# u and z of a chunked gMLP layer by seven block products, with v's norm moved into the v stage

## The chip, the cores and the metric

The kernel runs on one core of a Trainium2 chip. The metric is the device time of the program in microseconds. The tensor engine (PE) multiplies, VectorE (DVE) and ScalarE (ACT) do elementwise work, GpSimd (POOL) a few small steps, and SyncE (SP) issues the DMAs. The arrays live in three large tiles: arF (float32) and arR (float32r, the operands of matmuls) on chip, and arP, the eight PSUM banks of 512 columns.

## The reference

Two layers work on 128 prompt and 512 sample tokens (640 in all) of width 1024. The first is latent attention, the second, which the change touches, a gMLP mixer of width 2048:

```python
def chunk_mlp(h, w_in, v_g, v_b, w_s, b_s, w_o):
    b, t, _ = h.shape
    proj = h @ w_in
    uv = jax.nn.gelu(proj[..., :2 * MLP_WIDTH])
    z = proj[..., 2 * MLP_WIDTH:]
    u, v = uv[..., :MLP_WIDTH], uv[..., MLP_WIDTH:]
    v = layernorm(v, v_g, v_b).reshape(b, t // CHUNK, CHUNK, MLP_GROUPS, MLP_WIDTH // MLP_GROUPS)
    s = jnp.einsum('gpq,bcqgd->bcpgd', w_s, v) + b_s.T[:, :, None]
    return gated_out(u * s.reshape(b, t, MLP_WIDTH), z, w_o)
```

`gated_out(o, z, w_o)` is `(o * silu(z)) @ w_o`. What it gives is scaled by the modulation's gate, added to x, and the final RMS norm makes the outputs.

## The kernel before

Every float32 product is made of three float32r products: an operand x is split into h, x rounded (a CAST on ACT, line 134), and l, the exact rest (a subtraction on DVE, line 135), and `mm3` (lines 139 to 141) adds h·h, h·l and l·h into one PSUM bank. The tokens are five tiles of 128 (t), the input features eight tiles of 128 (k).

In the second layer h^T lies split in arR (R_HT). The **v stage** makes v in four column blocks c of 512 and five token tiles: `v_tile` runs 24 matmuls of 512 columns, ACT the gelu (L991), SP stores the block to DRAM (d_v), and DVE takes its statistics (L993). Mean and rstd (mv) of all tiles follow at the stage's end.

Then the **u/z stage** runs over 16 feature tiles f. `f_tile(f)` loads v's 128 columns from d_v, normalizes them in five steps of 128 (L1063) and splits them; `mix_s` multiplies them by the spatial weights of group f // 2 (ten matmuls of 256, L1085 and L1086: h and l of the weights side by side) and adds the halves with gain and bias on ACT and DVE (L1098 to L1104). `load_uz` loads and splits the 1024 x 128 weights of u and of z, `uz_mm` makes each of them, transposed (features by tokens), with 48 matmuls of 320 columns: eight k, two token halves, three products. gelu(u) (L1111), s u (L1113), z's tanh and z (1 + tanh) (L1115, L1116) and their product (L1120) give one tile of t^T, which is split into one of five slots.

The **output projection** is cut into four `out_quarter`s of four feature tiles each: after f = 4, 8, 12, and at the end. Each quarter sums its own k in PSUM (512 columns, two banks per token tile), and a DVE addition (L1166) carries the sum in arF. In the last quarter the gated residual, the squares and the final norm follow tile by tile; the last token tile comes in columns 512, 256 and 256.

All DMAs are issued by SP in one queue. Each engine runs its instructions in a fixed order; that order is set by the framework's scheduler, which moves ready work ahead of the order of the source, and semaphores make an instruction wait for its operands and for buffers still in use.

## Time and profile before

| what | us |
|---|---|
| median of three runs | 852.37 |
| their span | 851.84 to 853.99 |
| the profiled execution: its span | 851.1 |
| of it PE busy | 831.5 |
| DVE busy | 566.2 |
| ACT busy | 357.1 |
| u/z stage begins | 489.75 |
| last matmul begins | 843.33 |

The span is from the first to the last instruction of the profiled execution; the trace has no other time of that execution. Busy times of an engine are sums over its instructions. A matmul's listed duration runs into that of the next, so the distance between two starts tells what one costs. "Idle before" is the time an engine stood still ahead of a group, with what ended it.

### The profile page before, as it was taken

The page shows a single profiled execution, that of the slowest core. Times are in us where ns is not written, and L with a number is a line of the kernel's source. Part 1 is how long each engine was busy: PE and PEld are TensorE (multiplying, and loading weights), DVE is VectorE, ACT ScalarE, POOL GpSimd, SP SyncE. Part 2 cuts the span into 40 slices and gives each one's busy share as a digit, 9 for nine tenths or more (in the row PEclk, how much of TensorE's full clock was granted, in tenths as well). Part 3 has the DMA queues.
Part 4 walks back from the last instruction along what each step waited for, and adds up shares of the span by engine and source line. Part 5 has one row for each costly group of instructions (what it writes and reads, how often), then busy time and mean ns, then how long its engine had stood idle before and what let it go on. Part 6 is the DMA issues. An engine that isn't in the chain of part 4 may idle for free.

```text
span 851.1 us, 12612 instructions
## 1 busy us (share of the span) xinstructions
PE 831.5 (98%) x5030; PEld 763.2 (90%) x5030; DVE 566.2 (67%) x989; ACT 357.1 (42%) x597; POOL 17.3 (2%) x32
## 2 busy tenths in 40 slices
...
GB/s 278 297 278 29 171 223 154 26 50 68 76 75 99 50 116 246 90 152 160 260 247 117 85 201 93 97 90 30 141 112 82 9 162 90 75 25 99 149 50 99
DMA packets 97441, 105.41 MB, mean 124 GB/s; under 512 B 4300, under 2 KB 73448, under 8 KB 97128
## 3 DMA queue, kind: packets, MB, share of 16 engines
...
## 4 chain that ended last, share of the span: by engine, by line
PE 92%; DVE 2%; DMA 2%; ACT 1%; issue 1%; POOL 1%; SPq 0%; POOLq 0%; ACTq 0%
PE arP L139 27%; PE arP L141 27%; PE arP L140 26%; PE arP L722 6%; PE arP L750 2%; PE arP L1085 1%; PE arP L1086 1%; DMA arF<-in_w_mod 1%; PE arP L485 1%; DMA arF<-in_x_sample 1%; PE arP L226 1%; PE arP L922 1%; DVE arF L475 1%; DVE arR L135 0%; ACT arF L308 0%
## 5 line engine op out<-in xcount | busy, mean ns | idle before, releaser
L139 PE MATMUL arP<-arR 128*128 128x320 f32 (+3 forms) x1340 | 454.0, 339 | 1.7 <-ACT arR L134 1.1
L140 PE MATMUL arP<-arR 128*128 128x320 f32 (+3 forms) x1340 | 452.3, 338 | 0.0
L141 PE MATMUL arP<-arR 128*128 128x320 f32 (+3 forms) x1340 | 451.6, 337 | 0.0
L139 PEld LDWEIGHTS arP<-arR 128*128 128x128 f32 x1340 | 251.7, 188 | 23.6 <-ACT arR L134 3.9
L141 PEld LDWEIGHTS arP<-arR 128*128 128x128 f32 x1340 | 251.6, 188 | 19.6 <-issue 0.8
L140 PEld LDWEIGHTS arP<-arR 128*128 128x128 f32 x1340 | 251.9, 188 | 18.4 <-DVE arR L135 0.7
L134 ACT CAST arR<-arF 128x1024 fp32r<-128x1024 f32 (+2 forms) x147 | 135.2, 930 | 284.8 <-PE arP L140 88.8
L135 DVE TENSOR_TENSOR arR<-arF,arR 128x1024 fp32r<-128x1024 f32 (+2 forms) x147 | 154.6, 1067 | 112.6 <-ACT arR L134 110.5
L475 DVE SCALAR_TENSOR_TENSOR arF<-arF,silc 128x512 f32<-128x512 f32 x112 | 77.8, 745 | 2.6 <-DMA arF<-in_w_mod 2.6
L135 DVE TENSOR_TENSOR arR<-arP,arR 128x512 fp32r<-128x512 f32 (+4 forms) x87 | 54.8, 678 | 11.7 <-ACT arR L134 11.5
L722 PE MATMUL arP<-arR 128*128 128x320 f32 (+1 forms) x360 | 54.5, 308 | 0.1
L134 ACT CAST arR<-arP 128x512 fp32r<-128x512 f32 (+4 forms) x87 | 46.0, 601 | 16.4 <-PE arP L141 8.9
L722 PEld LDWEIGHTS arP<-arR 128*128 128x128 f32 x360 | 51.9, 188 | 0.4 <-DVE arR L685 0.4
L738 ACT ACTIVATE arF<-arP,st 128x640 f32<-128x640 f32 (+1 forms) x40 | 28.0, 703 | 23.5 <-DVE st L737 22.7
L993 DVE BATCH_NORM_STATS2 arF<-arF 128x6 f32<-128x512 f32 x20 | 13.8, 690 | 30.9 <-ACT arF L991 30.9
L991 ACT ACTIVATE arF<-arP 128x512 f32<-128x512 f32 x20 | 12.0, 598 | 51.6 <-PE arP L141 43.6
L742 ACT ACTIVATE arF<-arF,st 128x640 f32<-128x640 f32 (+1 forms) x40 | 29.0, 743 | 2.1 <-DVE st L741 1.8
L734 DVE TENSOR_REDUCE st<-arP 128x1 f32<-128x640 f32 (+1 forms) x40 | 28.1, 709 | 1.7 <-PE arP L722 1.0
L1166 DVE TENSOR_TENSOR arF<-arP,arF 128x1024 f32<-128x1024 f32 x10 | 12.2, 1223 | 25.5 <-PE arP L141 25.3
L1063 DVE TENSOR_SCALAR arF<-arF,mv 128x128 f32<-128x128 f32 x80 | 21.9, 340 | 8.5 <-DMA arF<-d_v 7.2
L1085 PE MATMUL arP<-arR 128*128 128x256 f32 x80 | 19.9, 284 | 0.0
L1086 PE MATMUL arP<-arR 128*128 128x256 f32 x80 | 19.9, 283 | 0.0
(144 smaller groups left out, 538.5 us busy)
## 6 DMA issues: line engine op xcount, KB each, us to landing
arF<-in_mlp_w_in SPq DMA_DIRECT2D x48, 512.0 KB, 4.0
arF<-in_w_mod SPq DMA_DIRECT2D x40, 512.0 KB, 4.1
arF<-in_mlp_w_o SPq DMA_DIRECT2D x16, 512.0 KB, 4.2
d_v<-arF SPq DMA_DIRECT2D x20, 256.0 KB, 2.4
arF<-d_v SPq DMA_DIRECT2D x16, 320.0 KB, 3.1
arF<-in_x_sample SPq DMA_DIRECT2D x8, 512.0 KB, 5.1
arF<-in_w_mod SPq DMA_DIRECT2D x16, 256.0 KB, 6.3
arF<-in_attn_w_in SPq DMA_DIRECT2D x8, 512.0 KB, 5.1
```

Of the source, the lines that this page charges most:

```text
L134: S.copy(h, x)
L135: V.tensor_tensor(l, x, h.bitcast(F32), ALU.subtract)
L139: T.matmul(out, a[0], b[0], start=start, stop=False)
L140: T.matmul(out, a[0], b[1], start=False, stop=False)
L141: T.matmul(out, a[1], b[0], start=False, stop=stop)
L475: V.scalar_tensor_tensor(acc[:, c, :], w, sc, acc[:, c, :], ALU.mult, ALU.add)
L722: T.matmul(p[:, n0 : n0 + n], a[:, qs], b[:, c0 : c0 + n], start=s0, stop=s1)
L734: V.tensor_reduce(c[:, 0:1], sc, AX.X if q == 0 else AX.XY, ALU.max)
L738: S.activation(pv, sc, AF.Exp, bias=c[:, 0:1], scale=SCALE, accum_out=c[:, 1:2])
L742: S.activation(pr, pr, AF.Identity, scale=c[:, 2:3])
L1085: T.matmul(out, vh[0][:, t, :], ws, start=True, stop=False)
L1086: T.matmul(out, vh[1][:, t, :], ws, start=False, stop=True)
```

## The change

**Seven block products.** For one feature tile the 1024 x 128 weights of u and of z are the two block rows of a matrix, the two halves of k its block columns; h^T is cut into halves of k and halves of tokens (320). Strassen's scheme in Winograd's form makes the four result blocks from seven products of four k tiles each (`prod`, 12 matmuls of 320): A11, A12 and A22 of the weights, S1 to S4, sums of weights, against B11, B21, B22 of h^T and T1 to T4, sums of it. z comes out with its sign turned, which the factor -0.5 in the tanh and in the gate of the layer puts right. The sums S are made for each f in `prep` (one DVE pass of 1024, two of 512, and splits of 1024, 1024, 1024 and 512 on ACT and DVE); the sums T once, in `t_sums`, in the v stage's c = 2, from h^T, which `h_turn` now stores to DRAM (d_h) and `t_sums` reloads; `t_last` puts T4 into h^T's place. The result blocks are put together on ACT and DVE: copies x1 and x5 of PSUM, additions y, v, and into z. Three banks serve a feature tile, two tiles in turn.

**v's norm.** In c = 3 each token tile is normalized as soon as its statistics are there: `v_norm`, four blocks of 512 columns a tile, 20 in all, with ACT's scaling, the split into one of two buffers at R_VL, and a store of both parts, 512 KB, to d_vh. Blocks c = 0 to 2 are reloaded from d_v, the fourth is still on chip.

**The mixes.** Even feature tiles are mixed in the u/z stage, one in every second `f_tile`, from a reload of d_vh. Odd tiles are mixed in the output projection, at the steps that `MSTEP` lists. The gated products t^T go to DRAM (d_t; for odd f without the mixed s) and come back in `t_parts`, through three buffers, which for odd f multiplies s in, and splits.

**The output projection** has two column halves, each with k over all 16 feature tiles in PSUM: half A with five token tiles in five banks, step by step; half B with three token tiles at once and then one at a time, the last in columns 256 and 256. The additions into arF are gone. The norm's halves follow each half.

```diff
-R_T = 25600
-R_VL = 32000
-R_WS = [24576, 34560]
+R_T = 24576
+R_WS = 32256
+R_VL = 34304
+R_UZ = [10240, 17408]
+TT = [10240, 11520, 12800] + [17152 + 1280 * j for j in range(13)]
...
-    d_v = dr.tile([NT, P, 2048], F32, name="d_v")
+    d_v = dr.tile([NT, P, 1536], F32, name="d_v")
+    d_vh = dr.tile([NT, P, 16, 2, P], F32, name="d_vh")
+    d_h = dr.tile([KD, P, TOK], F32, name="d_h")
+    d_t = dr.tile([16, P, TOK], F32, name="d_t")
...
+                -0.5 if layer else 1.0,
...
+        nc.sync.dma_start(d_h[:, :, ts_].rearrange("k p n -> p k n"), h3)
...
-        nc.sync.dma_start(d_v[t, :, c * 512 : (c + 1) * 512], vt)
+        if c < 3:
+            nc.sync.dma_start(d_v[t, :, c * 512 : (c + 1) * 512], vt)
...
+    def v_norm(t, c, x):
+        a = R_VL + stage[0] % 2 * 1024
+        stage[0] += 1
+        S.activation(x, x, AF.Identity, bias=mv[:, t, 2:3], scale=mv[:, t, 1:2])
+        y = R(a, 1024).rearrange("p (f s n) -> p f s n", f=4, s=2)
+        split(y[:, :, 0, :], y[:, :, 1, :], x.rearrange("p (f n) -> p f n", f=4))
+        nc.sync.dma_start(
+            d_vh[t, :, 4 * c : 4 * c + 4].rearrange("p f s n -> p (f s n)"),
+            R(a, 1024).bitcast(F32),
+        )
...
+        V.tensor_tensor(t1, b11, b12, ALU.subtract)
+        V.scalar_tensor_tensor(t2, t1, -1.0, b22, ALU.mult, ALU.subtract)
+        V.tensor_tensor(t3, b22, b12, ALU.subtract)
+        V.scalar_tensor_tensor(t4f[:, k, :], t2, -1.0, b21, ALU.mult, ALU.subtract)
+        dst = R(R_T, 7680).rearrange("p (j k n) -> p k j n", j=3, k=4)[:, k]
+        split(dst[:, :, :HALF], dst[:, :, HALF:], F3(F_Y, 3 * HALF, a=3))
...
+        w = R_UZ[f % 2]
+        x = F(a, 2048)
+        s = F(F_X, 2048)
+        split(R(w, 1024), R(w + 1024, 1024), x[:, :1024])
+        V.tensor_tensor(
+            s[:, :1024].rearrange("p (a b) -> p a b", a=2),
+            x.rearrange("p (a b) -> p a b", b=512)[:, 0:4:3, :],
+            x[:, 1024:1536].unsqueeze(1).to_broadcast([P, 2, 512]),
+            ALU.add,
+        )
+        V.tensor_tensor(s[:, 1024:1536], s[:, 512:1024], x[:, :512], ALU.add)
+        V.tensor_tensor(s[:, 1536:], s[:, 1024:1536], x[:, 512:1024], ALU.add)
+        split(R(w + 4096, 1024), R(w + 5120, 1024), s[:, 1024:])
+        split(R(w + 2048, 1024), R(w + 3072, 1024), s[:, :1024])
...
+            if c == 2 and t < 4:
+                t_sums(t)
...
+            if c == 3:
+                v_stats(t)
+                x = F(F_Y + t % 2 * 1536, 1536)
+                nc.sync.dma_start(x, d_v[t])
+                for cc in range(3):
+                    v_norm(t, cc, x[:, cc * 512 : (cc + 1) * 512])
+                v_norm(t, 3, vt)
+                if t == 2:
+                    end = prep(0, False)
+    t_last()
+    end()
...
-        for t in range(NT):
-            V.tensor_scalar(
-                vl[:, t, :],
-                vl[:, t, :],
-                mv[:, t, 0:1],
-                mv[:, t, 1:2],
-                ALU.subtract,
-                ALU.mult,
-            )
-        va = R_VL + (f % 2) * 1280
-        vh = R3(va, 640, a=NT), R3(va + 640, 640, a=NT)
-        split(vh[0], vh[1], vl)
...
+    def prod(out, f, a, b, first):
+        w = wuz[f][a]
+        for k in range(4):
+            h, l = [z[:, k * P : (k + 1) * P] for z in w]
+            H, L = MOV[b][k]
+            for j, (x, y) in enumerate(((h, H), (h, L), (l, H))):
+                T.matmul(
...
+    def mix_end(f):
+        s = mix_s(f)
+        V.tensor_tensor(s, s, wbuf(f), ALU.mult)
+        nc.sync.dma_start(d_t[f], s)
+    def f_tile(f):
+        a, b, c = [
+            arP[:, (f % 2 * 3 + j) * 512 : (f % 2 * 3 + j) * 512 + HALF] for j in range(3)
+        ]
+        u = F(2048 + (f % 2) * TOK, TOK)
+        z = F(3328 + (f % 2) * TOK, TOK)
+        x1, y, v, x5 = [F(4608 + (f % 2) * 1280 + j * HALF, HALF) for j in range(4)]
+        prod(a, f, "A11", "B11", True)
+        S.copy(x1, a)
+        prod(b, f, "S2", "T2", True)
+        V.tensor_tensor(y, b, x1, ALU.add)
+        prod(c, f, "S1", "T1", True)
+        S.copy(x5, c)
+        prod(a, f, "A12", "B21", False)
+        S.activation(u[:, NH[0]], a, AF.Gelu_apprx_tanh)
+        prod(b, f, "S3", "T3", False)
+        V.tensor_tensor(v, b, x1, ALU.add)
+        V.tensor_tensor(z[:, NH[1]], v, x5, ALU.add)
+        prod(c, f, "S4", "B22", False)
+        V.tensor_tensor(y, c, y, ALU.add)
+        S.activation(u[:, NH[1]], y, AF.Gelu_apprx_tanh)
+        if f % 2:
+            mix_mm(f - 1, 0, 4, 6)
+        prod(b, f, "A22", "T4", False)
+        V.tensor_tensor(z[:, NH[0]], b, x1, ALU.add)
+        if f % 2:
+            mix_mm(f - 1, 4, 5, 6)
+            mix_end(f - 1)
+        th = F(8448, TOK)
+        S.activation(th, z, AF.Tanh, scale=-0.5)
+        V.scalar_tensor_tensor(z, th, 1.0, z, ALU.add, ALU.mult)
+        V.tensor_tensor(wbuf(f), u, z, ALU.mult)
+        if f % 2:
+            nc.sync.dma_start(d_t[f], wbuf(f))
...
-                    V.tensor_tensor(m, p, m, ALU.add)
...
+            prep(1)
+        if f % 2 == 0:
+            mix_load(f)
+        f_tile(f)
+        if 0 < f < 15:
+            prep(f + 1)
...
+    def t_parts(j):
+        f = MIX[j]
+        x = F(F_X + j % 3 * TOK, TOK)
+        nc.sync.dma_start(x, d_t[f])
+        if f % 2:
+            V.tensor_tensor(x, x, mix_s(f), ALU.mult)
+        tT[j] = R(TT[j], TOK), R(TT[j] + TOK, TOK)
+        split(tT[j][0], tT[j][1], x)
...
+    MSTEP = {0: 0, 1: 1, 2: 2, 4: 3, 5: 4, 7: 5, 8: 6, 10: 7}
+    for j in range(16):
+        if j < 8:
+            t_parts(j)
+        wa[j] = wo_load(MIX[j], 0, (WE if j < 11 else WA)[j % 6])
+        m = MSTEP.get(j)
+        if m is not None:
+            mix_load(2 * m + 1)
+            mix_last(2 * m + 1)
+            t_parts(8 + m)
+        for t in range(NT):
+            mo_mm(PA[t], t, j, wa[j])
...
+    PA = [arP[:, b * 512 : (b + 1) * 512] for b in (0, 1, 2, 3, 5)]
...
+    PB = [arP[:, b * 512 : b * 512 + 512] for b in (4, 6, 7, 0, 1)]
+    for j in range(16):
+        for t in range(3):
+            mo_mm(PB[t], t, j, wb[j])
...
+            parts = [(0, 256, PB[t][:, :256]), (256, 512, arP[:, 1024:1280])]
+        for j, (n0, n1, q) in enumerate(parts):
+            if t >= 3:
+                for k in range(16):
+                    mo_mm(q, t, k, [z[:, n0:n1] for z in wb[k]])
```

What the rows below show is VectorE's order. The names arF, arR and arP are the three large tiles, mv the columns of mean and rstd, cst constants.

VectorE at the end of the v stage, before: L993 and L1015 are the statistics of a token tile, L135 splits.

```order
L135 TENSOR_TENSOR arR<-arF,arR 128x1024 x3
L993 BN_STATS arF<-arF 128x6
L1015 BN_AGGR mv<-arF 128x2
L135 TENSOR_TENSOR arR<-arF,arR 128x1024
L1016 TENSOR_SCALAR mv<-mv 128x5
L1063 TENSOR_SCALAR arF<-arF,mv 128x128 x9
L135 TENSOR_TENSOR arR<-arF,arR 128x640
L1063 TENSOR_SCALAR arF<-arF,mv 128x128
L135 TENSOR_TENSOR arR<-arF,arR 128x640
L135 TENSOR_TENSOR arR<-arF,arR 128x1024
```

VectorE at the same place, after: L1024 to L1027 are the statistics' last steps, L144 the splits (128x4x128 a chunk of v's norm, 128x1024 and 128x512 weights), L1081 to L1089 sums of weights.

```order
L1024 BN_AGGR mv<-arF 128x2
L144 TENSOR_TENSOR arR<-arF,arR 128x1024
L144 TENSOR_TENSOR arR<-arF,arR 128x4x128
L1025 TENSOR_SCALAR mv<-mv 128x1
L144 TENSOR_TENSOR arR<-arF,arR 128x1024
L1027 TENSOR_SCALAR mv<-mv 128x1
L144 TENSOR_TENSOR arR<-arF,arR 128x512
L1081 TENSOR_TENSOR arF<-arF 128x1024
L144 TENSOR_TENSOR arR<-arF,arR 128x4x128
L1088 TENSOR_TENSOR arF<-arF 128x512
L1089 TENSOR_TENSOR arF<-arF 128x512
L144 TENSOR_TENSOR arR<-arF,arR 128x4x128 x2
```

Where steps of 128 columns of v's norm began the u/z stage, chunks of it now stand among splits and sums of the first feature tiles' weights: the 128x4x128 rows are the tenth and eleventh chunk of twenty, and, in the last row, the twelfth and thirteenth.

VectorE in one feature tile of the u/z stage, before:

```order
L1063 TENSOR_SCALAR arF<-arF,mv 128x128 x5
L135 TENSOR_TENSOR arR<-arF,arR 128x1024
L1113 TENSOR_TENSOR arF<-arF 128x640
L135 TENSOR_TENSOR arR<-arF,arR 128x1024
L1116 SCALAR_TENSOR_TENSOR arF<-arF,arP 128x640
L1100 TENSOR_TENSOR arF<-arF 128x640
L1120 SCALAR_TENSOR_TENSOR arF<-arF 128x640
L1101 SCALAR_TENSOR_TENSOR arF<-arP,cst,arF 128x512
L1104 SCALAR_TENSOR_TENSOR arF<-arP,cst,arF 128x128
L135 TENSOR_TENSOR arR<-arF,arR 128x640 x2
L1089 SCALAR_TENSOR_TENSOR arF<-arF,cst 128x128
```

VectorE in an odd feature tile of the u/z stage and its neighbours, after: L1248, L1254, L1255, L1257 and L1262 put the blocks together, L1268 and L1269 apply z, L1220 and L1228 are the mix.

```order
L1269 TENSOR_TENSOR arF<-arF 128x640
L1248 TENSOR_TENSOR arF<-arP,arF 128x320
L1089 TENSOR_TENSOR arF<-arF 128x512
L144 TENSOR_TENSOR arR<-arF,arR 128x1024
L1254 TENSOR_TENSOR arF<-arP,arF 128x320
L1255 TENSOR_TENSOR arF<-arF 128x320
L144 TENSOR_TENSOR arR<-arF,arR 128x1024
L1257 TENSOR_TENSOR arF<-arP,arF 128x320
L1220 SCALAR_TENSOR_TENSOR arF<-arP,cst,arF 128x512
L144 TENSOR_TENSOR arR<-arF,arR 128x1024
L1228 SCALAR_TENSOR_TENSOR arF<-arP,cst,arF 128x512
L1262 TENSOR_TENSOR arF<-arP,arF 128x320
```

The five steps of v's norm and the split of t are gone from the stage; three splits, three sums of weights and five additions of blocks stand there.

VectorE around an output quarter, before: L1166 adds a token tile's sum, L135 splits the weights.

```order
L135 TENSOR_TENSOR arR<-arF,arR 128x640
L1166 TENSOR_TENSOR arF<-arP,arF 128x1024 x4
L135 TENSOR_TENSOR arR<-arF,arR 128x1024 x3
L1166 TENSOR_TENSOR arF<-arP,arF 128x1024
L1100 TENSOR_TENSOR arF<-arF 128x640
L135 TENSOR_TENSOR arR<-arF,arR 128x640
L1101 SCALAR_TENSOR_TENSOR arF<-arP,cst,arF 128x512
L1104 SCALAR_TENSOR_TENSOR arF<-arP,cst,arF 128x128
L1089 SCALAR_TENSOR_TENSOR arF<-arF,cst 128x128
```

VectorE in half A, after: L1220 and L1228 are the mix of an odd tile, L1295 multiplies s in, L144 splits reloaded tiles (128x640) and weights (128x512).

```order
L144 TENSOR_TENSOR arR<-arF,arR 128x640
L1295 TENSOR_TENSOR arF<-arF 128x640
L1210 SCALAR_TENSOR_TENSOR arF<-arF,cst 128x128 x2
L144 TENSOR_TENSOR arR<-arF,arR 128x512
L144 TENSOR_TENSOR arR<-arF,arR 128x640
L144 TENSOR_TENSOR arR<-arF,arR 128x512
L144 TENSOR_TENSOR arR<-arF,arR 128x640
L144 TENSOR_TENSOR arR<-arF,arR 128x512
L144 TENSOR_TENSOR arR<-arF,arR 128x640
L1220 SCALAR_TENSOR_TENSOR arF<-arP,cst,arF 128x512
L1220 SCALAR_TENSOR_TENSOR arF<-arP,cst,arF 128x128
L1228 SCALAR_TENSOR_TENSOR arF<-arP,cst,arF 128x512
```

The additions from PSUM are gone, and the mix's steps stand between the splits that the next steps' matmuls take.

## Rows read from the trace of the kernel before

**Rows 1.** The page's first section: busy us, share of span, instructions.

```profile
PE 831.5 (98%) x5030; PEld 763.2 (90%) x5030; DVE 566.2 (67%) x989; ACT 357.1 (42%) x597; POOL 17.3 (2%) x32
```

**Rows 2.** PE's waits: total us, times, longest.

```profile
PE arP L301 <- DVE arF L294: 9.1, 1, 9.1
PE arP L139 <- ACT arR L134: 1.1, 1, 1.1
PE arP L139 <- DVE arR L135: 0.6, 2, 0.4
```

**Rows 3.** Busy us by stretch; the columns stand in its first line.

```profile
core 0: us, PE busy (x) PEld busy (x) DVE busy (x) ACT busy (x) POOL busy (x), PEclk, DMA share, GB/s
400.00:489.75 89.75, 89.75 (x410) 74.47 (x409) 48.14 (x68) 26.85 (x34) 0.00 (x0) 1.00 0.58 181
489.75:843.60 353.85, 353.85 (x2189) 335.12 (x2187) 203.90 (x304) 113.33 (x156) 4.32 (x10) 1.00 0.31 93
509.00:532.00 23.00, 23.00 (x160) 22.91 (x160) 18.23 (x36) 7.86 (x11) 0.00 (x0) 1.00 0.34 96
...
843.60:847.00 3.40, 0.01 (x1) 0.00 (x0) 2.05 (x7) 2.08 (x8) 1.74 (x2) 1.00 0.38 154
847.00:851.10 4.10, 0.00 (x0) 0.00 (x0) 0.47 (x1) 0.44 (x1) 0.00 (x0) 0.59 0.34 128
```

**Rows 4.** PE's timeline, 320 to 512 columns: start us, duration us, engine, line.

```profile
559.74 0.31 PE L139 MATMUL arP<-arR 128*128 128x320 f32 x1
...
566.34 0.39 PE L139 MATMUL arP<-arR 128*128 128x512 f32 x1
```

**Rows 5.** PE's timeline, where the 120 matmuls of 512 end.

```profile
593.33 0.39 PE L141 MATMUL arP<-arR 128*128 128x512 f32 x1
593.56 0.28 PE L1085 MATMUL arP<-arR 128*128 128x256 f32 x1
```

**Rows 6.** PE's timeline, the ten matmuls of 256 of one mix.

```profile
520.50 0.28 PE L1085 MATMUL arP<-arR 128*128 128x256 f32 x1
...
521.69 0.31 PE L139 MATMUL arP<-arR 128*128 128x320 f32 x1
```

**Rows 7.** DVE by line and shape: busy us, mean ns, idle before, releasers.

```profile
L135 DVE TENSOR_TENSOR arR<-arF,arR 128x1024 fp32r<-128x1024 f32 x89 | 107.7, 1220 | 105.1 <-ACT arR L134 103.3
L135 DVE TENSOR_TENSOR arR<-arF,arR 128x640 fp32r<-128x640 f32 x47 | 37.4, 817 | 6.5 <-ACT arR L134 6.4
L135 DVE TENSOR_TENSOR arR<-arP,arR 128x512 fp32r<-128x512 f32 x51 | 32.3, 679 | 0.2 <-ACT arR L134 0.2
L1063 DVE TENSOR_SCALAR arF<-arF,mv 128x128 f32<-128x128 f32 x80 | 21.9, 340 | 8.5 <-DMA arF<-d_v 7.2 <-POOL mv L1017 1.3
L993 DVE BATCH_NORM_STATS2 arF<-arF 128x6 f32<-128x512 f32 x20 | 13.8, 690 | 30.9 <-ACT arF L991 30.9
L1101 DVE SCALAR_TENSOR_TENSOR arF<-arP,cst,arF 128x512 f32<-128x512 f32 x16 | 11.9, 745 | 0.0
L1104 DVE SCALAR_TENSOR_TENSOR arF<-arP,cst,arF 128x128 f32<-128x128 f32 x16 | 5.5, 342 | 0.0
L135 DVE TENSOR_TENSOR arR<-arP,arR 128x256 fp32r<-128x256 f32 x6 | 2.5, 417 | 0.1
```

**Rows 8.** DVE's timeline, instructions that wait for nothing.

```profile
536.91 1.23 DVE L135 TENSOR_TENSOR arR<-arF,arR 128x1024 fp32r<-128x1024 f32 x1 [3.80 <-ACT arR L134]
538.05 0.81 DVE L1116 SCALAR_TENSOR_TENSOR arF<-arF,arP 128x640 f32<-128x640 f32 x1
538.78 0.82 DVE L1100 TENSOR_TENSOR arF<-arF 128x640 f32<-128x640 f32 x1
```

**Rows 9.** ACT by line and shape, columns as in rows 7.

```profile
L134 ACT CAST arR<-arF 128x1024 fp32r<-128x1024 f32 x89 | 93.4, 1052 | 226.7 <-PE arP L140 88.8 <-PE arP L141 55.1 <-issue 31.1
L134 ACT CAST arR<-arF 128x640 fp32r<-128x640 f32 x47 | 34.1, 730 | 51.5 <-DVE arF L1120 29.2 <-DVE arF L320 16.1 <-DVE arF L1063 4.2
L134 ACT CAST arR<-arP 128x512 fp32r<-128x512 f32 x51 | 27.4, 609 | 2.1 <-PE arP L750 1.2 <-PE arP L141 0.9
L1111 ACT ACTIVATE arF<-arP 128x640 f32<-128x640 f32 x16 | 11.2, 699 | 3.7 <-PE arP L141 3.7
L1098 ACT ACTIVATE arF<-arP,cst 128x512 f32<-128x512 f32 x16 | 10.9, 684 | 0.3 <-PE arP L1086 0.3
L1099 ACT ACTIVATE arF<-arP,cst 128x128 f32<-128x128 f32 x16 | 5.9, 367 | 0.0
```

**Rows 10.** DMA issues: KB each, median us to landing; last, d_x: min/median/max.

```profile
d_v<-arF SPq DMA_DIRECT2D x20, 256.0 KB, 2.4
arF<-d_v SPq DMA_DIRECT2D x16, 320.0 KB, 3.1
d_x<-arF SPq DMA_DIRECT2D x5, 512.0 KB, 3.1
arF<-d_x SPq DMA_DIRECT2D x5, 512.0 KB, 3.2
DMA to landing us min/median/max: 2.7/3.2/4.3
```

**Rows 11.** The timeline behind the last matmul.

```profile
843.41 1.38 POOL L1209 TENSOR_TENSOR arF<-arF 128x512 f32<-128x512 f32 x1 [0.71 <-DVE arF L1179]
843.72 0.42 DVE L1178 TENSOR_TENSOR arF<-arP,arF 128x256 f32<-128x256 f32 x1
844.17 0.90 DVE L1179 TENSOR_TENSOR arF<-arF 128x256 f32<-128x256 f32 x1
```

360 lines of the change are left out of this document (179 added, 181 removed).

## The prediction

> **What bounds the kernel now.** I read the page's first section, the waits of the tensor engine (PE), a table by stretches, then starts in the timeline. PE is busy for 831.5 of 851.1 us [rows 1]; its largest wait, 9.1 us, stands at the start [rows 2], which the change leaves alone. In the stretch that it rewrites, from 489.75 us (first u/z matmul) to 843.60 us, PE is busy for 353.85 us of 353.85, VectorE (DVE) for 203.90, ScalarE (ACT) for 113.33, at a granted clock of 1.00 [rows 3]. So the matmuls there are the time, and taking some away pays in full for as long as the others keep up. Even in 509 to 532 us, where DVE works 18.23 us of 23, PE has no gap [rows 3].
>
> A matmul's price is the distance between starts, since its listed duration overlaps the next. 320 columns: 45 from 559.74 to 566.34, 0.1467 us [rows 4]. 512 columns: 120 from 566.34 to 593.56, 0.2268 [rows 4, 5]. 256 columns: ten from 520.50 to 521.69, 0.119 [rows 6]. The stretch holds 1536, 468 and 184 of them: 225.3 + 106.1 + 21.9 = 353.4, against 353.85 read. The prices hold.
>
> **1. The matmuls.** u and z need 84 matmuls per feature tile for 96, 192 fewer in all: -28.2. The output projection's last tile now runs in 256 columns throughout (36 matmuls of 512 become 72 of 256): -8.2 + 8.6 = +0.4. Together -27.8. Weight loads per matmul stay one.
>
> **2. The tail.** Now 843.60 to 851.1. The 512-wide product on POOL from 843.41, 1.38 us, goes, and with it what it costs the DVE product beside it, 0.90 us for 256 columns at 844.17, where the reading of PSUM just ahead took 0.42 for as many [rows 11]. I take -0.6, between 0 and -1: the chain of square, sum, rstd, two scalings and store stays. Floor without any stall: 851.1 - 27.8 - 0.6 = 822.7.
>
> **3. First seam, v to u/z.** v's norm moves from DVE steps of 128 columns [rows 7], which PE never waited for [rows 2], to 20 chunks of 512: on ACT a scaling (0.684) and a CAST (0.609), on DVE a subtraction (0.679), then a store of 512 KB [rows 7, 9, 10]. Chunks share two buffers, so two chunks take CAST 0.61 + subtraction 0.68 + issue 0.33 + landing. For the landing I take 3.1, the median of the 512 KB stores of d_x; 2.7 and 4.3 are the ends of the transfers of that size [rows 10]. That is 4.72 a pair, 2.36 a chunk (2.16 to 2.96). By the order on DVE, eight chunks are subtracted when the V stage ends, and twelve are left. Up to the twelfth, DVE has a subtraction of 1280 (1.5, by the rows of 640 and 1024), one bn_stats (0.69), three subtractions of 1024 (3.66), one of 512 (0.68), four chunks (2.72), the weight sums of 1024, 512 and 512 (2.58) and some columns (0.56): 12.4 us by the rows' durations [rows 7], 11.2 at the spacing of step 4.
> PE has work meanwhile: three products each for feature tiles 0 and 1. Tile 0's fourth product overwrites a bank that ACT must first copy to x1, and x1 lies on the last v tile of token tile 2, so it waits for the twelfth chunk. Behind it other products hang on chunks 13, 16, 17, 18; tile 1's fourth product, the thirteenth in PE's order, hangs on chunk 19. Chunk 19 comes at 12.4 + 7 x 2.36 + copy 0.5 = 29.4 us, PE has 12 products x 12 x 0.1467 = 21.1 us of work by then: a stall of 8.3 (5.7 at the short landing and spacing, 12.5 at the long). The queues of ACT and SP that the stores and norms share can only add: I take 9.
>
> **4. Steady u/z.** Two feature tiles are 168 x 0.1467 + 10 x 0.119 = 25.8 us of PE. DVE gets eight passes of 1024, six of 512, ten of 320 (not in the trace; 0.48 between the rows of 256 and 512), five of 640 and the mix's two of 512 and three of 128: 9.8 + 4.1 + 4.8 + 4.1 + 2.5 = 25.2 us by durations. But an instruction that waits for nothing starts before the listed end of the one ahead: 1.14 after a 1.23, 0.73 after 0.81 and 0.82 [rows 8]. At such spacing it is 22.5, 87% of PE's time. ACT needs 12.8: six CASTs of 1.052, two of 0.609, eight passes of 320 at some 0.48, between its rows of 128 and 512, and two of 0.70 [rows 9]. DVE keeps a reserve of 0.6 to 3.3 us a pair, and by the order nearly all of PE's waits are on results that DVE has done at least 1 us before. I take 1 us over all eight pairs, 0 to 4.
> The Trainium skill (VectorE: DVE Perf Modes, "The DRAIN you can't avoid") says that the next DVE operation doesn't start until the pipe is empty, and adds that one that isn't held starts earlier. By the first half DVE would be full at 25.2 of 25.8; these rows side with the second.
>
> **5. Second seam, u/z to the first half of the output projection.** Eight odd mixes move here. Each costs DVE two passes of 512, three of 128, a 640 product and a 640 subtraction: 1.49 + 1.02 + 1.64 = 4.15 us. In the first eleven k steps DVE has 8 x 4.15 + 8 x 0.82 (even tiles) + 11 x 0.68 (weights) = 47.3 us, PE 11 x 15 x 0.2268 + 80 x 0.119 = 46.9: no reserve. Three reload buffers serve sixteen tiles, so a reload (3.1, [rows 10]) waits for its predecessor's subtraction, then CAST 0.73 and subtraction 0.82 follow: 4.65 against a step of 3.40. Some five steps lie open to this by 1.25 each: 6.2. I take 6; 2 if the queue of DVE runs ahead from the last u/z products, 9 if the mix that follows a mix on one bank waits as well.
>
> **6. At nothing.** The d_h stores and reloads, the sums of the moving side and the two early weight sets fall into the V stage, where DVE has 41.6 of 89.75 us free and ACT 62.9 [rows 3]; they add some 26 on DVE (four sums of 3.1, eight chunks of 0.68, one weight set of 6.9, t_last 1.5). Without that room they would cost what overflows. The sign in the gate and the split tail of the last norm hang on nothing that PE waits for.
>
> **Sum.** 822.7 + 9 + 1 + 6 = 838.7, against a span of 851.1. The median of the runs is 852.37, 1.3 above this span; so 840.0, 12.4 us (1.5%) faster.
>
> **Rivals.** (a) *The seams are covered.* For it: chunks drain earlier than I reckon in the V stage, where stores landed in 2.4 us for 256 KB [rows 10]. Then the seams cost 2 to 4 instead of 15: 822.7 + 1 + 3 + 1.3 = 828.
> (b) *The clock falls in the first seam.* The trace: with PE idle from 843.60 the granted clock was still 1.00 to 847.00, then 0.59 (near 1.2 of 2.4 GHz) to the end [rows 3]; the seam's waits are 2 to 4 us each, close together. At the lower level a product takes 3.5 us for 1.76; three or four that are not hidden in stalls add 6: 846.
> The Trainium skill (TensorE: Matmul & The Clock Gate, "What's actually happening") says that the throttled state is the default and activity releases it; the trace agrees at its end, and no row shows stalls of this kind in the middle.
> (c) *Slower: DVE becomes the bound in u/z.* In the row of 1024-wide subtractions DVE idles 103.3 us for ACT's cast in 89 cases, 1.16 each [rows 7]. If in each pair three of its eight splits idle so while nothing else can run, a pair is 25.2 + 3.5 = 28.7, that is 2.9 x 8 = 23 more: 863. It decides against the change from 25.8 + 12.4 / 8 = 27.4 a pair. Against it: the order puts other DVE work between cast and subtraction nearly everywhere.
>
> **How the numbers follow.** My case: 0.61. Rival (a) 0.20, (b) 0.10, (c) 0.09. What a measurement can tell from no change is about 0.3%, 849.8 to 854.9. Ends of my own case: 822.7 + (5.7 + 0 + 2) + 1.3 = 831.7 and 822.7 + (12.5 + 4 + 9) + 1.3 = 849.5, so it is nearly all faster (0.58), as is (a), and of (b) 0.07: 0.85. Within 0.3%: 0.02 + 0.03 + 0.02 of (c) = 0.07; 0.08 slower with the rest of (c) and the seams at their worst. The range leaves out about 0.2: 828, the centre of (a), to 855, past (b) and up to where (c) begins.
>
> **What would show it.** In the changed kernel's table by stretches PE should be busy throughout between the seams, with u/z pairs of 25.8 to 26.2 us; the waits should name ACT's copy of x1 and x5 in the first 30 us after the V stage (some 9 us) and the splits of reloaded tiles in the first half of the output projection (some 6). Waits of PE on DVE that recur in every pair would be (c); a granted clock under 0.9 behind the first seam (b); PE waits under 8 us beyond the start's, (a). If the matmul starts stand further apart than 0.1467 us, step 1 itself is wrong.

## The result and the profile after

The changed kernel takes 860.25 us (median of four runs, 857.14 to 862.30) against 853.18 for the kernel before, whose runs are now four as well: 1.0081 of its time, 95% interval 1.0054 to 1.0109. Run again later, beside another set of the kernel before, it gave 862.98 and 1.013 (1.0096 to 1.0163). It is slower by 0.8 to 1.3%; 840.0 was forecast, 828 to 855. The profiled execution is the fastest of the four, 857.14 us with a span of 855.4, so the accounts below are made against that span. One run below, of the kernel with a product moved to GpSimd, was slow (896.14 us at a mean granted clock of 0.85, the other three 842.06 to 844.50): that kernel's median counts it, its ratio does not.

The page's first section after, for [rows 1]:

```profile
PE 814.8 (95%) x4874; PEld 743.4 (87%) x4874; DVE 641.3 (75%) x1135; ACT 403.1 (47%) x692; POOL 18.1 (2%) x31
```

156 matmuls and 16.7 us of busy PE are gone, and yet the span is 4.3 us longer. PE's waits after (us in total, times, longest), for [rows 2], where 1.7 us stood beyond the start's:

```profile
PE arP L310 <- DVE arF L303: 9.2, 1, 9.2
PE arP L148 <- ACT arR L143: 8.5, 3, 3.9
PE arP L1169 <- ACT arF L1246: 4.8, 1, 4.8
PE arP L1169 <- ACT arF L1252: 3.0, 1, 3.0
PE arP L1205 <- DMA arR<-d_vh: 1.9, 2, 1.3
PE arP L1205 <- DVE arF L1228: 1.5, 1, 1.5
PE arP L1169 <- DVE arR L144: 1.3, 1, 1.3
PE arP L1169 <- ACT arF L1250: 1.2, 1, 1.2
```

By stretches, for [rows 3], with the same columns: the first seam, the steady u/z stage, the second seam.

```profile
500.00:510.00 10.00, 5.20 (x28) 4.90 (x28) 6.00 (x9) 5.11 (x8) 1.41 (x1) 0.79 0.90 291
510.00:520.00 10.00, 5.78 (x22) 4.98 (x21) 3.54 (x5) 5.67 (x9) 0.00 (x0) 0.67 0.86 305
520.00:530.00 10.00, 10.00 (x59) 9.60 (x59) 7.33 (x12) 6.22 (x11) 0.00 (x0) 0.86 0.45 181
...
560.00:690.00 130.00, 130.00 (x898) 129.95 (x897) 120.16 (x178) 63.23 (x93) 0.00 (x0) 1.00 0.49 147
...
712.00:764.00 52.00, 42.55 (x210) 35.73 (x209) 38.84 (x69) 16.09 (x26) 0.00 (x0) 0.90 0.80 256
```

Between 560 and 690 us PE is full at clock 1.00. The loss lies at both ends of u/z: in the first seam 28 and 22 matmuls stand in ten us each, where 68 of 320 columns would fit, and the DMA share is 0.86 to 0.90 against 0.34 in the same place before; the second has PE busy 42.55 us of 52.

**How much each seam loses.** The starts of the stage's first matmul, of the output projection's first and of its last bound both seams:

```profile
489.76 5.44 PE L1169 MATMUL arP<-arR 128*128 128x320 f32 x36
...
714.96 0.39 PE L148 MATMUL arP<-arR 128*128 128x512 f32 x1
...
848.11 0.28 PE L150 MATMUL arP<-arR 128*128 128x256 f32 x1
```

At the prediction's prices the u/z stage holds 1344 x 0.1467 + 80 x 0.119 = 206.7 us, the output projection 432 x 0.2268 + 176 x 0.119 = 118.9. So the first part loses 714.96 - 489.76 - 206.7 = 18.5 us, the second 848.11 - 714.96 - 118.9 = 14.2. Behind the last matmul stand 7.3 us, for 7.8 before. With the floor of the prediction, 822.7 + 18.5 + 14.2 = 855.4, the whole span. The experiments are measured by these two losses; one profiled execution each, while the ratio comes from timed runs. The second loss of the repeat was 17.3 (the first 18.3), so a difference of 3 us in it is not yet a finding. The runs below show how far each loss scatters by itself: the six profiled executions that leave the first seam as it is lose 18.3 to 22.5 there, the six that leave the second as it is 14.2 to 18.4.

**What each seam waits for.** The chain of waits after in the first seam: start, duration, piece.

```profile
499.84 5.77 DMA d_vh<-arR
...
505.69 0.63 ACT arR L143
...
506.34 0.70 DVE arR L144
...
507.12 0.43 ACT arF L1246
...
507.60 3.32 PE arP L1169 x11
...
513.87 3.08 DMA d_vh<-arR
...
518.95 5.45 PE arP L1169 x24
```

A chunk's store lands, its buffer's next user is cast and subtracted, ACT may copy x1, PE goes on. But the chain also runs the other way: from 507.05, where the twelfth store is issued, to the last store at 529.42 it holds one landing only, the 3.08 us, and two stretches of PE's own products, 3.32 and 5.45 us. Behind these stand the CASTs, splits and additions of the feature tiles, which come ahead of the next chunk in the orders of ACT and DVE.

At the end of the seam stands a step that I had left out, the first mix. The last store is issued at 529.42, and the reload follows its landing:

```profile
529.42 2.83 DMA d_vh<-arR
...
532.32 5.87 DMA arR<-d_vh
```

PE's timeline has the mix right behind it:

```profile
538.24 0.38 PE L1205 MATMUL arP<-arR 128*128 128x256 f32 x1 [1.34 <-DMA arR<-d_vh]
```

The reload does not wait for its data. Feature tile 0 lies in the first chunk of each token tile; the last of these is chunk 17, stored at 521.41 and landed 2.6 us later. The reload waits for its place: it goes to R_VL, where the two chunk buffers lie, and so it waits for the last user of both. In the version below that has no chunk buffers and six slots the reloads are issued as soon as chunk 17, the first of the last four stores, has landed (3.1 us), and before the other three have. A place of its own for the reload was not tried by itself. SP's timeline of that version:

```profile
502.32 2.45 SPq L1014 DMA_DIRECT2D d_vh<-arF  x4
505.42 1.02 SPq L1185 DMA_DIRECT2D arR<-d_vh  x2
```

The second seam in the chain of waits: a mix's two passes on DVE, the split behind them that frees a reload slot, the reload of a t tile into it, its CAST, and PE.

```profile
722.51 1.01 DVE arF L1220 x2
723.52 0.74 DVE arR L144
724.28 5.12 DMA arF<-d_t
729.42 0.73 ACT arR L143
730.20 0.50 PE arP L148
```

### The profile page after: what moved, and what is told of

It is laid out like the page before. It is cut to its first block, busy times and chain, and to the rows that moved or that the text cites. A ratio compares the mean times of both kernels' runs of the same rounds, so it can differ in the third digit from the quotient of the medians.

```text
span 855.4 us, 12734 instructions
## 1 busy us (share of the span) xinstructions
PE 814.8 (95%) x4874; PEld 743.4 (87%) x4874; DVE 641.3 (75%) x1135; ACT 403.1 (47%) x692; POOL 18.1 (2%) x31
## 4 chain that ended last, share of the span: by engine, by line
PE 80%; DMA 7%; DVE 6%; ACT 3%; issue 2%; POOL 1%; SPq 0%; POOLq 0%; ACTq 0%; DVEq 0%
PE arP L1169 21%; PE arP L148 16%; PE arP L150 15%; PE arP L149 15%; PE arP L735 6%; DVE arR L144 2%; PE arP L763 2%; DMA d_vh<-arR 2%; DMA arF<-d_h 1%; DMA arF<-d_t 1%; ACT arR L143 1%; PE arP L1205 1%; PE arP L1206 1%; ACT arF L1015 1%; PE arP L235 1%
## 5 line engine op out<-in xcount | busy, mean ns | idle before, releaser
L148 PE MATMUL arP<-arR 128*128 128x512 f32 (+3 forms) x840 | 299.6, 357 | 9.1 <-ACT arR L143 8.5
L149 PE MATMUL arP<-arR 128*128 128x512 f32 (+3 forms) x840 | 297.6, 354 | 0.0
L150 PE MATMUL arP<-arR 128*128 128x512 f32 (+3 forms) x840 | 295.9, 354 | 0.0
L143 ACT CAST arR<-arF 128x1024 fp32r<-128x1024 f32 (+4 forms) x204 | 168.8, 844 | 208.6 <-PE arP L1169 41.8
L144 DVE TENSOR_TENSOR arR<-arF,arR 128x1024 fp32r<-128x1024 f32 (+4 forms) x204 | 193.1, 962 | 61.1 <-ACT arR L143 59.5
L1169 PE MATMUL arP<-arR 128*128 128x320 f32 x1344 | 206.1, 314 | 10.7 <-ACT arF L1246 4.8
L1169 PEld LDWEIGHTS arP<-arR 128*128 128x128 f32 x1344 | 201.7, 191 | 12.9 <-ACT arF L1246 5.1
L148 PEld LDWEIGHTS arP<-arR 128*128 128x128 f32 x840 | 158.7, 189 | 30.8 <-ACT arR L143 11.7
L150 PEld LDWEIGHTS arP<-arR 128*128 128x128 f32 x840 | 158.7, 189 | 19.8 <-issue 0.8
L149 PEld LDWEIGHTS arP<-arR 128*128 128x128 f32 x840 | 158.8, 189 | 17.9 <-DVE arR L144 0.7
L144 DVE TENSOR_TENSOR arR<-arP,arR 128x512 fp32r<-128x512 f32 (+4 forms) x86 | 54.8, 686 | 11.4 <-ACT arR L143 11.2
L735 PEld LDWEIGHTS arP<-arR 128*128 128x128 f32 x360 | 51.9, 188 | 0.4 <-DVE arR L698 0.4
L1350 DVE TENSOR_TENSOR arF<-arP,arF 128x512 f32<-128x512 f32 (+1 forms) x11 | 6.8, 638 | 33.2 <-PE arP L150 33.2
L1352 ACT ACTIVATE arF<-arF 128x512 f32<-128x512 f32 (+1 forms) x11 | 6.5, 589 | 45.4 <-DVE arF L1351 45.4
L1250 ACT COPY arF<-arP 128x320 f32<-128x320 f32 x16 | 6.8, 424 | 36.7 <-PE arP L1169 36.0
L155 POOL TENSOR_TENSOR st<-st,nhalf 128x1 f32<-128x1 f32 x15 | 10.1, 673 | 658.8 <-DVE st L154 331.9
```

The costliest lines, as they stand in the source:

```text
L143: S.copy(h, x)
L144: V.tensor_tensor(l, x, h.bitcast(F32), ALU.subtract)
L148: T.matmul(out, a[0], b[0], start=start, stop=False)
L149: T.matmul(out, a[0], b[1], start=False, stop=False)
L150: T.matmul(out, a[1], b[0], start=False, stop=stop)
L735: T.matmul(p[:, n0 : n0 + n], a[:, qs], b[:, c0 : c0 + n], start=s0, stop=s1)
```

## The experiments

The rivals for the first seam: the chain of v's chunks through two buffers, their store and reload; the bytes moved; the time at the lower clock; the queue that issues the stores. For the steady stage: DVE as its bound. For the second seam: the three reload slots, the transfers, DVE's mix passes. "Loss" below is the pair of numbers just defined, 18.5 and 14.2 for the changed kernel.

**Half the bytes of v's store and reload.** Only the first half of the split is stored and read.

```diff
-        split(y[:, :, 0, :], y[:, :, 1, :], x.rearrange("p (f n) -> p f n", f=4))
+        split(R(a, 512), R(a + 512, 512), x)
...
-            R(a, 1024).bitcast(F32),
+            R(a, 512).bitcast(F32),
```

> The changed kernel, in which v's norm stores and reloads only the high part h of v: 256 KB a chunk for 512, 320 KB a feature tile for 640. The low part is left out of the mix (h is multiplied twice instead), so the values differ; ACT, DVE and PE do the same number of instructions. Theory A (the chain of chunks through two buffers, each waiting for its store to land, at a DMA share near 1.0, sets the end of the first seam): the last eleven stores, which now take 29.6 us (499.8 to 529.4), come some 2.0 us apart instead of 2.96 and the reload behind them lands in 4 for 5.9, so the first seam falls from 18.6 us lost to about 8, the second by 2 to 4 of 14.2; some 12 us less than the changed kernel. Theory B (the fall of the clock is the cost, the transfers are hidden): within 3 us of the changed kernel.

855.66 us, 1.0038 (1.0023 to 1.0053); losses 14.7 and 14.1. Half the bytes give back 3.8 of the 18.5, between the two figures expected. The chain of waits shows why it is no more: the store at which PE hangs took 6.26 us with 256 KB.

```profile
499.34 6.26 DMA d_vh<-arR
```

A reload of 768 KB (d_v) had been issued at 498.59, 0.75 us ahead of it. The store's own size does not set its landing here.

**PE kept at work in the first seam.** 50 matmuls of no use, 7.3 us, stand in the second feature tile's order.

```diff
+        if f == 1:
+            fill(30)
...
+        if f == 1:
+            fill(20)
```

> The changed kernel with 50 extra matmuls of 320 columns into an unused bank, in three groups (18, 12, 20) where PE stands still in the first seam; they cost 7.3 us of PE if nothing hides them. Theory B (the clock): with PE kept at work the granted clock stays at 1.00 through the seam, products there take 1.76 us and not 3.57, and the kernel gets some 4 to 6 us faster. Theory A (the chunk chain): the clock stays up but the waits behind the chunks and the mix that waits for the last of them at 538.2 us end when they did; within 1.5 us of the changed kernel. If the groups are too long for the waits: up to 3 us slower.

860.81, 1.0088 (1.0065 to 1.0111); the first seam loses 20.2 with the fills in it, the second 15.6. The fills held the clock up until 520 us (for 0.79 and 0.67 after), but not behind it (for 0.86), as the stretches show; the last line is from PE's timeline:

```profile
500.00:510.00 10.00, 7.75 (x50) 7.46 (x49) 6.46 (x10) 5.17 (x9) 1.46 (x1) 0.96 0.87 289
510.00:520.00 10.00, 7.84 (x46) 7.58 (x44) 2.43 (x3) 5.20 (x8) 0.00 (x0) 0.87 0.59 229
520.00:530.00 10.00, 8.11 (x43) 7.84 (x44) 5.30 (x10) 4.27 (x8) 0.00 (x0) 0.83 0.59 209
...
521.30 5.33 PE L1169 MATMUL arP<-arR 128*128 128x320 f32 x24 [3.46 <-ACT arF L1259]
```

The kernel didn't get faster. But the test doesn't settle what the clock costs. In the chain of waits the fills stand twice, with 2.78 us (510.36) and 2.95 us (514.91); ACT's gelu that lets the next products start began at 520.81, for 518.46 in the changed kernel; PE waited 3.46 us for it, the clock fell again, and the 24 matmuls that took 5.45 us in the changed kernel took 5.33.

**Six reload slots for three.**

```diff
+    SLOT = [0, 640, 1280, 2048, 2688, 3328]
...
-        x = F(F_X + j % 3 * TOK, TOK)
+        x = F(SLOT[(j < 8) * 3 + j % 3], TOK)
```

> The changed kernel with six buffers for the reloaded tiles instead of three: the first eight steps of half A and the odd tiles have three each. Theory A2 (in the second seam an even tile's reload waits for the buffer of an odd tile, behind its mix): PE's two waits of 3.4 and 3.9 us on the splits, and the clock's falls behind them (some 3.4 us), go: 8 to 10 us faster than the changed kernel. Theory C (VectorE's work itself, 47.3 us against 46.9 of PE, or the transfers' bandwidth, sets the second seam): the waits move to other instructions and the kernel gains under 3 us.

856.02, 1.0038 (1.0014 to 1.0061); losses 19.5 and 9.6. The slots are worth 4.6 us of the second seam, and not all of it: less than one theory expected, more than the other. With the four kernels below that also have six slots and all mixes on DVE, 9.2 to 11.2 us are lost there, clear of the 14.2 to 18.4 without.

**A third buffer for v's chunks.**

```diff
-        a = R_VL + stage[0] % 2 * 1024
+        n = stage[0] % 3
+        b = F(9472, 1024).bitcast(F32R) if n == 2 else R(R_VL + n * 1024, 1024)
```

> The changed kernel with a third buffer for the chunks of v's norm. If the first seam is the latency of two buffers, a chunk's cadence falls from 2.96 us toward 2.2 and the seam by some 7 us. If it is the bandwidth of the DMA engines (9.8 MB in 32 us, 306 GB/s, share 0.88), landings lengthen by as much and the gain is under 2 us. The second seam is unchanged.

850.93, 0.998 (0.9966 to 0.9994); losses 9.3 and 17.3. One more buffer takes 9.2 us out of the first seam: the last store is issued at 517.75 instead of 529.42. What is left is store and reload, in the chain of waits of this kernel:

```profile
517.75 4.70 DMA d_vh<-arR
...
522.53 6.54 DMA arR<-d_vh
```

**v stored whole, split when it is read back.** The chunk goes to memory straight from the tile that the norm has scaled; no buffer, half the bytes, but a copy on ACT and a subtraction on DVE for each feature tile later.

```diff
-        split(y[:, :, 0, :], y[:, :, 1, :], x.rearrange("p (f n) -> p f n", f=4))
...
+        nc.sync.dma_start(l.bitcast(F32), d_vh[:, :, f].rearrange("t p n -> p t n"))
+        S.copy(h, l.bitcast(F32))
+        V.tensor_tensor(l, l.bitcast(F32), h.bitcast(F32), ALU.subtract)
```

> The changed kernel, in which v's norm stores the normalized block itself (256 KB) and the split into h and l is made at the reload, one CAST of 640 on ACT and one subtraction of 640 on VectorE per feature tile: no chunk buffers, 12 x 0.69 us less VectorE in the first seam, half the bytes of d_vh. Theory A (the chunk chain with the landing of its stores): the chain has one store less per pair and no buffer to wait for; the first seam falls from 18.6 us lost to 5 to 8, the second by up to 3: some 12 us less than the changed kernel. Theory D (VectorE, 25.2 us by durations of 25.86 a pair, has no room): the added 0.8 us a pair turns the u/z stage into one that VectorE bounds, pairs of over 26.2 us, and eats 3 us or more of that.

844.32, 0.9903 (0.9882 to 0.9924); losses 6.9 and 15.9. Without the chunks' buffers 11.6 us of the first seam are gone; with them went the splits of the seam, half the bytes, and the wait of the reload for the buffers' place. The work that moved into the pairs cost nothing there.

**That, and six reload slots.** The two edits together.

> The kernel of e5_xstore with the six reload buffers of e3_slots. If the two seams are independent, the gain of e3_slots (4 to 5 us in the second seam) adds to that of e5_xstore: some 16 us less than the changed kernel, 844. If both live on the same DMA bandwidth, less than 2 us comes on top.

841.68, 0.9858 (0.9838 to 0.9878); losses 5.7 and 11.2. The seams are independent: both gains are there. Of the versions that do the whole work this one has the lowest median, 1.4% ahead of the kernel before; two variants of it below, 843.18 and 842.57, are not apart from it. Its waits, of which the start's 9.0 are as before:

```profile
PE arP L310 <- DVE arF L303: 9.0, 1, 9.0
PE arP L1164 <- ACT arF L1242: 3.3, 1, 3.3
PE arP L148 <- ACT arR L143: 3.0, 3, 1.4
PE arP L1201 <- ACT arR L1186: 2.3, 1, 2.3
```

It also tells of the rival in the steady stage. Its pairs stand as close as those after, by the starts of two mixes in PE's timeline (25.89 us apart, 25.85 after), though each asks DVE for one subtraction of 128 x 640 (0.82 us) more than after:

```profile
517.91 0.28 PE L1201 MATMUL arP<-arR 128*128 128x256 f32 x1
...
543.80 0.28 PE L1201 MATMUL arP<-arR 128*128 128x256 f32 x1
```

**v's stores issued by GpSimd.**

```diff
-        nc.sync.dma_start(
+        nc.gpsimd.dma_start(
```

> The changed kernel, with the twenty stores of v's norm issued from GpSimd, so in another DMA queue than SyncE's loads. Theory E (one queue is served in order, so a store lands late because it stands behind the loads of 512 and 768 KB issued ahead of it: 5.8 us at 499.84 behind a load issued at 498.36): the stores land in about 3 us, the first seam loses 6 to 9 us less. Theory F (the sixteen DMA engines' bandwidth, share 0.9 to 1.0, whatever the queue): landings stay, under 2 us gained; slower if issuing from GpSimd costs more than SyncE's 0.33 us.

872.97, 1.0241 (1.0212 to 1.027); losses 27.6 and 18.4. That the stores lose time behind the others in SP's queue is not borne out: from a queue of their own they land later, by the DMA issues (count, size, median us to landing), 3.4 for 2.9 after. The second line is one store alone, issued at 497.64, 0.27 us behind SP's reload of 768 KB from d_v:

```profile
d_vh<-arR POOLq DMA_DIRECT2D x20, 512.0 KB, 3.4
...
d_vh<-arR POOLq DMA_DIRECT2D x1, 512.0 KB, 6.6
```

The stores at 484.44 and 512.37, as close behind such a reload, took 6.6 and 6.7 us. So a store is late beside a large load in another queue as well. (GpSimd also makes a step of v's statistics, between its stores in its order; what share that has in the 27.6 I did not separate.)

**A third buffer and six slots.**

> The changed kernel with the third chunk buffer of e4_stage3 and the six reload buffers of e3_slots. Their gains stand in different seams (9.4 us in the first, 4.6 in the second): if they add, 860 - 14 = 846. If the second seam's transfers move with the first and collide, 850.

844.44, 0.99 (0.9867 to 0.9932); losses 8.1 and 11.1. Here too both gains add up.

**The odd mixes left out of the output projection.**

```diff
-        if f % 2:
-            V.tensor_tensor(x, x, mix_s(f), ALU.mult)
...
-            mix_load(2 * m + 1)
-            mix_last(2 * m + 1)
```

> The changed kernel without the eight odd mixes in half A: their reloads of v, 80 matmuls (9.5 us of PE), VectorE's passes and the products with s are left out, the odd tiles go unmixed into the projection. The reloads of t^T through three buffers stay. Theory A2 (the buffers and the landing of these reloads set the second seam): the waits on the splits of reloaded tiles remain, and the kernel is about 9.5 us faster than the changed one, plus up to 4. Theory C (VectorE's work, 4.15 us for each odd tile, sets it): the second seam's 14.2 us lost go to 2 to 4, so 20 us faster.

834.52, 0.9782 (0.9745 to 0.9818); losses 19.7 and 1.0, the second against its own 109.4 us of matmuls. From 700 to 850 us PE has no wait at all. So all but 1 us of the second seam hangs on the mixes: on their reloads, their matmuls or their DVE passes.

**The reloads of v for these mixes left out**, the mixes run on what lies in the buffer.

```diff
+        if f % 2 == 0:
             nc.sync.dma_start(
                 R3(R_VL + b * 1280, 1280, a=NT).bitcast(F32),
```

> The changed kernel without the reloads of v for the eight odd mixes (640 KB each, 5 MB in the second seam); the mixes multiply what the buffer still holds, so the values differ, all other instructions stay. If these transfers set the second seam (they share the DMA engines with the reloads of t^T), it loses 8 us less than the changed kernel's 14.2; if VectorE's passes do, under 3 us less. The first seam stays within 2 us.

861.79, 1.01 (1.0074 to 1.0126); losses 22.5 and 13.3. Not these reloads: the second seam stays, 0.9 us below the lowest of the unchanged ones. (The first has the same chain of waits there; the 24 matmuls on it took 5.73 us, and the reload at its end 7.28 for 5.87.)

**The odd mixes' passes moved from DVE to ACT**, one plain scaling for two passes, with other values.

```diff
+        if f % 2:
+            S.activation(s, p4[:, :, 1, :], AF.Identity, scale=gcol)
+            return
```

> The changed kernel in which the odd mixes' four VectorE passes over PSUM (2 x 0.745 and 2 x 0.342, 2.2 us of the 4.15 of a tile) are replaced by one pass of 512 and one of 128 on ACT (0.68 and 0.37); the high parts and the bias are left out, so the values differ. If VectorE's work sets the second seam, it loses 7 to 11 us less than 14.2; if the transfers do, under 3 us less.

856.21, 1.0037 (1.0015 to 1.0059); losses 20.0 and 8.8. The stretch of the second seam shows 7.5 us less on DVE, 4.4 more of PE and the clock at 0.97:

```profile
712.00:764.00 52.00, 46.92 (x241) 39.60 (x241) 31.36 (x49) 25.52 (x44) 0.00 (x0) 0.97 0.81 263
```

So the passes on DVE are worth 5.4 us against the changed kernel's profile, which has the lowest loss of the unchanged seams, with three slots and all transfers in place.

**Three edits that moved little.** On the best version: the first feature tile's x1, y and v moved off v's tile,

```diff
-        x1, y, v, x5 = [F(4608 + (f % 2) * 1280 + j * HALF, HALF) for j in range(4)]
+        x1, y, v, x5 = [
+            F((4608 + (f % 2) * 1280 if f else 9472) + j * HALF, HALF) for j in range(4)
+        ]
+        if f == 0:
+            x5 = F(4608 + 3 * HALF, HALF)
```

> The kernel of e7_xs_slots with x1, y and v of feature tile 0 in words of their own instead of on the last v block of token tile 2. PE's first wait of the seam, 3.3 us for ACT's copy to x1, which waits for that block's store, goes; the products behind it then wait for later blocks. If the first block to come free sets the seam: 3 us less than e7_xs_slots (some 839). If the chain's end sets it (the mix that needs all blocks): under 1 us.

and that with 16 matmuls of no use in the second seam (2.35 us):

```diff
+        if j == 1:
+            fill(16)
```

> The kernel of e12_reloc with 16 extra matmuls of 320 columns (2.35 us) into an unused bank ahead of the third odd mix, where PE stands still some 2.7 us in the second seam and its clock falls to half behind that. If the clock costs time there, 1.5 to 2 us less than e12_reloc; if VectorE and the transfers set the end of the seam, the same within 1 us.

On the changed kernel, the weights of later feature tiles not loaded (14 MB less):

```diff
-        for j in range(2):
+        for j in range(2 if f < 2 else 0):
```

> The changed kernel in which the feature tiles from 2 on take the weights of tiles 0 and 1, so that 14 MB of weight loads are left out (the values differ); every other instruction stays. Theory G (the stores of v's norm land late because the weight loads share the DMA engines): landings in the first seam fall from 3 to 6 us toward 2.6, and the seam loses 4 to 8 us less. Theory H (the two buffers and the landing without company set it): within 3 us of the changed kernel. The second seam is unchanged by it.

With the buffers moved: 843.18, losses 6.6 and 9.6, no gain over the best version's 841.68. With the fills besides: 842.57, losses 5.6 and 9.2 beyond the fills; this doesn't tell what the clock costs there, because the fills ran at 718.64, behind the wait and the fall of the clock:

```profile
710.00:716.00 6.00, 4.90 (x15) 4.07 (x16) 5.52 (x10) 2.17 (x3) 0.00 (x0) 0.50 0.88 271
```

Without the loads, on the changed kernel: 856.37, 1.0029 (1.0014 to 1.0045), losses 15.5 and 16.0; these loads are worth some 3 us of the first seam.

**The odd product moved to GpSimd**, on the best version.

```diff
-            V.tensor_tensor(x, x, mix_s(f), ALU.mult)
+            G.tensor_tensor(x, x, mix_s(f), ALU.mult)
```

> The kernel of e7_xs_slots with the eight products of odd tiles with s on GpSimd instead of VectorE (0.82 us each there, 6.6 in all; on GpSimd some 1.7 each, by the 1.38 that 512 columns took in the kernel before). If VectorE's work sets the second seam, its loss falls from 11.2 us by 2 to 5, to some 838; if the longer product on GpSimd stands in the chain of a tile's reload, the same or 2 us slower than e7_xs_slots.

844.29, 0.9903 (0.9884 to 0.9923); losses 5.0 and 12.0. DVE is rid of 0.82 us a mix, but the product now takes 2.16 (by line: count, then busy us and mean ns) in the same chain:

```profile
L1292 POOL TENSOR_TENSOR arF<-arF 128x640 f32<-128x640 f32 x8 | 17.3, 2157 | 244.3 <-DMA d_t<-arF 208.6 <-DVE arF L1224 35.7
```

**The changed kernel again**, unedited; its time stands in the section on the result.

> The changed kernel itself, unchanged, on the chip of these runs. 860 us, first seam 18.5 us lost, second 14.2, by every theory.

## Why the prediction was wrong

**Step 1, the matmuls: right.** PE's timeline after has the mixes of successive pairs at

```profile
557.13 0.28 PE L1205 MATMUL arP<-arR 128*128 128x256 f32 x1
...
582.97 0.28 PE L1205 MATMUL arP<-arR 128*128 128x256 f32 x1
```

25.84 us apart; the five pairs to 686.39 take 25.85 on the mean, and 25.8 was reckoned. With the losses set aside, the floor of 822.7 closes the account to 0.1 us. The 27.8 us were gained and then lost at the seams.

**Step 2, the tail: right.** 7.8 us became 7.3; -0.5 for -0.6.

**Step 4, the steady stage: right, with 0 for 1 us.** Rival (c) falls with it, though its 863 is the nearest of my numbers to the time; that is luck, since it counted 23 us in a stage that lost none. DVE was busy 120.16 us of 130, 23.9 a pair, between the 22.5 and the 25.2 reckoned, and PE waited for nothing. In the best version a pair with one DVE subtraction more kept its length: by the prediction's durations that is 25.2 + 0.82 = 26.0 us of DVE in the 25.89 that the pair took, so durations are not the measure. That is also where the Trainium skill was weighed (VectorE: DVE Perf Modes, "The DRAIN you can't avoid"); the trace after agrees with the second half of what it says, with a split that starts 0.41 us behind the start of an addition listed at 0.50 (525.02).

**Step 3, the first seam: the failed step, 9 forecast and 18.5 lost.** I ended the seam at chunk 19 and the product that hangs on it. That product waited for nothing: the 108 matmuls from 518.95 run without a gap. The three waits that PE had, 4.8, 3.0 and 1.2 us behind ACT's copies and gelu, add to the 9 that I forecast, but that is luck: they stand ahead of chunk 19's product, and the loss is twice as much. The seam ends at the first mix, which waits for chunk 20 to leave its buffer, then for a reload of 640 KB. With that step, and the 5.4 us that such a reload took after, my numbers would have given 12.4 + 8 x 2.36 + 0.7 for the last issues + 3.1 landing + 5.4 reload - 204 x 0.1467 of matmuls = 10.6. The other 8 us are start and cadence.

The twelfth store came 4.9 us later than reckoned. The store at 499.84, which took 5.77 us instead of 3.1, is 2.7 of that. The rest stands with chunks 7 and 8, which I had read as done when the v stage ends (489.76) and which were stored from 492.47 on. The eight intervals from there (507.05) to the last (529.42) are 2.80 each for 2.36, 3.5 more; last landing and reload were 0.4 shorter than in that sum.

So, besides the step left out, two terms were wrong. In the start the landing was mis-sized: I took the median of the stores of d_x, elsewhere in the kernel [rows 10], and here the stores share the DMA engines (share 0.86 to 0.90) with reloads of v and loads of weights. In the cadence the path was wrong: I made it of CAST, subtraction, issue and landing alone, and the chain of waits spends 8.77 of these 22.4 us on PE's products and 3.08 on a landing. The products wait for chunks, and the chunks wait, in the orders of ACT and DVE, for work that hangs on the products. The DMA issues after give for these transfers:

```profile
d_vh<-arR SPq DMA_DIRECT2D x20, 512.0 KB, 2.9
arR<-d_vh SPq DMA_DIRECT2D x16, 640.0 KB, 5.4
...
arF<-d_t SPq DMA_DIRECT2D x16, 320.0 KB, 4.5
```

A median of 2.9 looks as assumed; the one on which the chain hung first is the slow one. A third buffer, with nothing else changed, gave 9.2 us back; no buffer, with the other things that this changed, 11.6; half the bytes 3.8, a quieter DMA 3.0. What hurt most was that two buffers tie a chunk to the chunk two before it. A store is slow for the loads in flight beside it: the one of 5.77 us had 512 KB of weights issued 1.5 us before it and the one of 6.26 us 768 KB. The store of the same tenth chunk took 3.3 us instead of 5.77 in the kernel without the later weight loads, and the last four of the changed kernel, from 521.41 on and with no load issued since 514.24, took 2.6 to 2.83. GpSimd's stores show that it doesn't take one queue's order.

**Rival (b), the clock: it fell as described, and what it cost stays open.** PE's timeline after has a product of twelve matmuls, 1.76 us at full clock, in 3.57:

```profile
507.60 3.57 PE L1169 MATMUL arP<-arR 128*128 128x320 f32 x12 [4.80 <-ACT arF L1246]
512.36 3.57 PE L1169 MATMUL arP<-arR 128*128 128x320 f32 x12 [1.19 <-ACT arF L1250]
518.95 17.95 PE L1169 MATMUL arP<-arR 128*128 128x320 f32 x108 [3.02 <-ACT arF L1252]
```

Added up, the seam's listed waits are 12.0 us and these slower matmuls make most of the other 6.5, about the 6 that the rival priced. Two stretches of them lie on the chain of waits, 11 matmuls in 3.32 us and 24 in 5.45, which is 3.6 us more than at 0.1467 each. So up to 3.6 us of this seam may be the clock's; how much of it a full clock would give back is not shown, since the fills came onto the chain and the clock fell again behind them. In the second seam no run held the clock up without taking work away.

**Step 5, the second seam: the failed step as well, 6 forecast, 14.2 and 17.3 lost in two executions.** The statement that DVE had no reserve (47.3 us against PE's 46.9; its terms add to 47.2) stood in the text, and I priced it only as five gaps of latency at a reload of 3.1 us. The reloads on the chain took 5.12 (724.28) and 5.61 (745.24). With 5.4, their mean, the loop is 5.4 + 0.73 + 0.82 = 6.95 against 3.40, and five such gaps are 17.7, near what was lost. Yet the latency alone is not it: six slots gave 4.6 back, taking the passes off DVE 5.4, taking the mixes away 13.2. The loop runs through both, DVE's passes delay the split that frees the slot, and the slot delays the reload. How the 14 us divide between them, and what the lower clock behind these waits has in it, stays open; both edits in one kernel were not tried. The reloads of v set little of it (13.3 without them).

**Step 6: right.** The first matmul of u/z starts at 489.76 us, for 489.75 before: what was moved into the v stage cost PE nothing there.

**Rival (a), covered seams, falls** by 32.7 us lost for 4. The two mistakes add to 17.7 us (9.5 + 8.2), more than the 12.4 that I had forecast to gain; the long ends of my own case, 12.5 and 9, were drawn from landings elsewhere in the kernel and held neither.
